# One pair of w_down's block sums made in the up projection instead of beside the last heads, in a hybrid attention and feed-forward layer on Trainium2

## The chip, the cores and the metric

The kernel runs on one core of one Trainium2 chip. The metric is the device time of one execution in microseconds (us). A core has a matrix engine (PE), a vector engine (DVE), a scalar engine (ACT), GpSimd (POOL) and SyncE (SP), which here only issues DMA transfers. Each engine works through its own list of instructions in order and waits on semaphores; a transfer that SP issues runs on 16 DMA engines that all queues share.

## The reference

One layer over 256 positions of width 2048: an RMS norm, one wide projection `w_in` (queries, keys and values for 6 forgetting heads, 6 stick-breaking heads and 4 heads over a memory, and three gates), the heads, three branch products weighted by the gates, an output product, and a gated feed-forward with a causal convolution of three taps. All in float32.

```
proj = rms_norm(x, g_mix) @ w_in
merged = g0 * (o_fox @ w_br_fox) + g1 * (o_sb @ w_br_sb) + g2 * (o_mem @ w_br_mem)
x = x + merged @ w_out
u = causal_depthwise_conv(rms_norm(x, g_ffn) @ w_up, conv_w, conv_b)
u_gate, u_val = split(u);   x = x + (silu(u_gate) * u_val) @ w_down
```

## The kernel before

**Products.** Every weight arrives as float32 in pieces of 128 x 1024 (512 KB), which SP loads into one of four `raw` buffers. ACT rounds a piece to `hi` (line 143 or 379) and DVE makes the rest, `lo = raw - hi` (line 144 or 380); there are four `hi` and four `lo` buffers. PE multiplies with `hi` and `lo` (lines 385 to 387, and 1365 and 1366 in the up stage). A `raw` buffer is free for the load of the piece four later when `lo` of its own piece is made.

**Stages**, in order of time: the memory product `kv`, the projections `mq`, `f` and `s` with the heads between them, the branch products of the first half (`b`, with the last stick-breaking heads beside them), the gates (`g`), the branch products of the second half, `w_out` (`o`), `w_up` (`u`) and `w_down` (`d`).

**Block sums.** In `w_out` and `w_down` some pairs of k-tiles ("sevens", the letter `s` in the plans) are multiplied in seven block products instead of eight. These need sums of the weight's blocks, four per pair, which do not depend on the data. A stream makes them ahead of time: it loads a pair's weights (1 MB), DVE adds them (`sums_in`, lines 254 to 256), and the sums are stored to HBM as `kept_...`, from where the `o` and `d` stages load them. The pairs stand in one list, `halves`, and generators take them from its front: `first_sums` and `pair_sums_ahead` beside the projections (15 pairs), `half_sums` (half a pair at a time, a load of two times 256 KB, three DVE operations and a store of 512 KB) beside the branch products, and `pair_sums_ahead` in the up stage (whole pairs, 18 of them).

**The up stage.** `w_up` is read in 176 steps of one piece each; eight steps fill four banks, and the order of the groups is gate columns, value columns, gate columns, and so on. After each step's matmuls `tick()` moves the background generators by one. `DU` is the number of ticks before the first pair of sums, and the tuple handed to `pair_sums_ahead` (line 1274) gives the ticks from each pair's load to the next one's. A pair's sums are written one tick after its load and its store five ticks after it. All pairs of this stage use one buffer, `ends`, so that a load waits until the store before it has landed. In the first steps ACT and DVE also end the `w_out` stage, form the transposed hidden state `hT`, and make the row scale `rbc`: DVE line 637 gives `scales`, POOL sends it to HBM and back (lines 1233 and 1234), and DVE line 1310, the first operation of each convolution after its copies, reads it.

Of the kernel before, what the change touches and what calls it, by code (L numbers as in the profile page):

```python
# [10 lines left out]
F32 = mybir.dt.float32  # L11
# [5 lines left out]
P = 128  # L17
# [19 lines left out]
BLOCKS = 14  # L37
GS = 3
PF = (6, 5)
DU = 7  # L40


@with_exitstack
def hybrid_block(
# [76 lines left out]
    def until(*names):  # L121
        while not issued.issuperset(names):
            yield
# [128 lines left out]
    def sums_in(w):  # L252
        both = w[:, 1:2].to_broadcast([P, 2, w.shape[2]])
        in_order(nc.vector.tensor_tensor(w[:, 0:2], w[:, 0:4:3], both, ALU.add))
        in_order(nc.vector.tensor_tensor(w[:, T2], w[:, T1], w[:, T2], ALU.add))
        in_order(nc.vector.tensor_tensor(w[:, T4], w[:, T2], w[:, T4], ALU.add))

    def kept_for(name, nb, pr):
        if (name, nb, pr) not in sums_of:
            at = f"kept_{name}{nb}_{pr}"  # L260
            sums_of[name, nb, pr] = dram.tile([P, 4, 512], F32, tag=at, name=at)
        return sums_of[name, nb, pr]

    def half_sums(staging, period, add, store, starts):

        for start in starts:
            yield from until(*start)
            name, wv, nb, pr, h = halves.popleft()
            kept = kept_for(name, nb, pr)
            w = staging(f"pre_{name}{nb}_{pr}_{h}").rearrange("p (i c) -> p i c", i=4)  # L270
            n0 = nb * PIECE + h * 256
            for n in range(2):
                in_order(
                    nc.sync.dma_start(
                        w.rearrange("p (k n) c -> p k n c", k=2)[:, :, n],
                        wv[:, 2 * pr : 2 * pr + 2, n0 + n * 512 : n0 + n * 512 + 256],
                    )
                )
            for _ in range(add):
                yield  # L280
            sums_in(w)
            for _ in range(store - add):
                yield
            in_order(nc.sync.dma_start(kept[:, :, h * 256 : (h + 1) * 256], w))
            for _ in range(period - store):
                yield

    def pair_sums_ahead(staging, period, add, store, most=99, delay=0):

        due = deque()  # L290
        clock = 0
        for _ in range(delay):
            yield

        def step():
            while due and due[0][0] <= clock:
                _, kept, w = due.popleft()
                in_order(nc.sync.dma_start(kept, w))

        periods = cycle(period if isinstance(period, tuple) else (period,))  # L300
        while len(halves) > 1 and halves[0][-1] == 0 and most:
            most -= 1
            name, wv, nb, pr, _ = halves.popleft()
            halves.popleft()
            kept = kept_for(name, nb, pr)
            w = staging(f"pre_{name}{nb}_{pr}")
            in_order(
                nc.sync.dma_start(
                    w.rearrange("p (k c) -> p k c", k=2), wv[:, 2 * pr : 2 * pr + 2, nb * PIECE : (nb + 1) * PIECE]
                )  # L310
            )
            w = w.rearrange("p (i c) -> p i c", i=4)
            due.append((clock + store, kept, w))
            for t in range(next(periods)):
                if t == add:
                    sums_in(w)
                step()
                clock += 1
                yield
        while due:  # L320
            step()
            clock += 1
            yield
# [342 lines left out]
    gp = mix.enter_context(tc.tile_pool(name="gp", bufs=3))  # L666
# [407 lines left out]
    def x_sums():  # L1074
# [5 lines left out]

    background.append(x_sums())
    background.append(
        half_sums(lambda name: gp.tile([P, 1024], F32, tag="pre", bufs=1, name=name), 6, 2, 4, ((), (), ("second",), ()))
    )


# [165 lines left out]
    for nb, plan in enumerate(o_plans):  # L1252
# [18 lines left out]
    ends = []  # L1271
    ends_tile = lambda name, dt: ff.tile([P, 2, PIECE], dt, tag="ends", bufs=1, name=name)
    background.append(
        pair_sums_ahead(lambda name: ends_tile(name, F32).rearrange("p i c -> p (i c)"), (15,) + (8,) * 20, 1, 5, delay=DU)
    )
    a_done = []
    background.append(last_sums(148, 12))
# [72 lines left out]
    for f0 in range(0, FT, 4):  # L1350
# [5 lines left out]
        for s in range(2):  # L1356
            ps = [bank(f"u{f0 + i}_{s}") for i in range(4)]
            c0 = s * D_FF + f0 * P
            for k in range(0, KT, 2):
                hi, lo = piece(upv[:, k : k + 2, c0 : c0 + 512], 2, 512, f"u{f0}_{s}_{k}")  # L1360
                for j in range(2):
                    first, last = k + j == 0, k + j == KT - 1
                    for i in range(4):
                        c = slice(i * P, (i + 1) * P)
# [63 lines left out]
    for nb, plan in enumerate(d_plans):  # L1428
# [5 lines left out]
        for t in range(NT):  # L1434
            for n in range(2):
                c = nb * PIECE + n * 512
                o = xres[:, t, c : c + 512]
                nc.vector.tensor_tensor(o, o, X[t][n], ALU.add)
                if (nb, t, n) == (1, 1, 1):
                    nc.scalar.dma_start(ov[:, t, c : c + 256], o[:, :256])  # L1440
                    c, o = c + 256, o[:, 256:]
# [35 lines left out]
```

## Time and profile before

| | |
|---|---|
| time, median of 3 runs | 1453.27 us (1453.22 to 1453.76) |
| profiled execution | 1453.81 us, of which the span is 1452.1 us |
| PE, DVE, ACT busy | 1447.0, 1247.5, 870.1 us |
| up stage on PE | from about 737 us on, 176 steps |
| pairs of sums in the up stage | 18 loads of 1 MB and 18 stores of 1 MB |

The span is cut into engines' busy times; a row of the timeline gives start and duration in us, engine, source line, operation, and what it writes and reads. Matmuls are pipelined: their durations overlap, so the distance from start to start tells PE's pace. SPq is the issue of a transfer, not its run.

### The profile page before, as it was taken

The page shows a single profiled execution, that of the slowest core. Times are in us where ns is not written, and L with a number is a line of the kernel's source. Part 1 is how long each engine was busy: PE and PEld are TensorE (multiplying, and loading weights), DVE is VectorE, ACT ScalarE, POOL GpSimd, SP SyncE. Part 2 cuts the span into 40 slices and gives each one's busy share as a digit, 9 for nine tenths or more (in the row PEclk, how much of TensorE's full clock was granted, in tenths as well). Part 3 has the DMA queues.
Part 4 walks back from the last instruction along what each step waited for, and adds up shares of the span by engine and source line. Part 5 has one row for each costly group of instructions (what it writes and reads, how often), then busy time and mean ns, then how long its engine had stood idle before and what let it go on. Part 6 is the DMA issues. An engine that isn't in the chain of part 4 may idle for free.

```text
span 1452.1 us, 20709 instructions
## 1 busy us (share of the span) xinstructions
PE 1447.0 (100%) x7298; PEld 1225.8 (84%) x7298; DVE 1247.5 (86%) x1851; ACT 870.1 (60%) x1248; POOL 32.3 (2%) x70
## 2 busy tenths in 40 slices
PE   9999999999999999999999999999999999999998
PEld 7888888888888888888888888888888888888887
DVE  5888778777999999998897888888888877999988
ACT  6755445465555555546676656556556556676775
POOL 0000011010000000000000000000000011000000
PEclk9999999999999999999999999999999999999999
DMA  8797899775677676788877888888888899789996
GB/s 296 228 350 269 309 336 321 266 250 182 214 219 230 202 219 207 265 267 278 289 231 264 302 273 292 284 267 303 288 275 298 274 252 262 251 286 345 317 341 236
DMA packets 165783, 393.41 MB, mean 271 GB/s; under 512 B 12859, under 2 KB 28111, under 8 KB 161327
## 3 DMA queue, kind: packets, MB, share of 16 engines
q1 hardware_dynamic: 162190, 384.86, 79.3%
q0 software_dynamic: 2160, 5.12, 1.8%
q10 hardware_dynamic: 1328, 2.11, 0.4%
q8 instruction: 57, 0.93, 0.2%
q14 instruction: 48, 0.39, 0.1%
HBM read 353.24 MB, written 43.00 MB: 273 GB/s over the span
## 4 chain that ended last, share of the span: by engine, by line
PE 98%; DMA 1%; ACT 0%; DVE 0%; issue 0%; DVEq 0%; ACTq 0%
PE u L1365 22%; PE u L1366 11%; PE xg L387 5%; PE xg L386 5%; PE xg L385 5%; PE xd L387 3%; PE xd L386 3%; PE xd L385 3%; PE s L385 2%; PE s L387 2%; PE f L385 2%; PE f L386 2%; PE f L387 2%; PE s L386 2%; PE b L387 2%; PE b L386 2%
## 5 line engine op out<-in xcount | busy, mean ns | idle before, releaser
L1365 PE MATMUL u<-hT,hi_u 128*128 128x512 f32 x1232 | 428.4, 394 | 0.0
L1366 PE MATMUL u<-hT,lo_u 128*128 128x256 f32 x1232 | 341.3, 277 | 0.0
L1365 PEld LDWEIGHTS u<-hT,hi_u 128*128 128x128 f32 x1232 | 231.0, 188 | 53.6
L144 DVE TENSOR_TENSOR lo_u<-raw_u,hi_u 128x1024 fp32r<-128x1024 f32 x176 | 215.1, 1222 | 69.4 <-ACT hi_u L143 69.3
L143 ACT CAST hi_u<-raw_u 128x1024 fp32r<-128x1024 f32 x176 | 184.6, 1050 | 131.5 <-PE u L1365 105.1
L1366 PEld LDWEIGHTS u<-hT,lo_u 128*128 128x128 f32 x1232 | 231.3, 188 | 0.0
L379 ACT CAST hi_g<-raw_g 128x1024 fp32r<-128x1024 f32 (+1 forms) x96 | 92.5, 973 | 54.0 <-PE xg L386 23.7
L380 DVE TENSOR_TENSOR lo_d<-raw_d,hi_d 128x1024 fp32r<-128x1024 f32 x88 | 106.8, 1222 | 12.3 <-ACT hi_d L379 6.9
L379 ACT CAST hi_d<-raw_d 128x1024 fp32r<-128x1024 f32 x88 | 91.7, 1054 | 35.8 <-PE xd L386 12.2
L380 DVE TENSOR_TENSOR lo_g<-raw_g,hi_g 128x1024 fp32r<-128x1024 f32 (+1 forms) x96 | 106.4, 1119 | 4.1 <-ACT hi_g L379 3.6
L385 PE MATMUL xg<-hi_g,xT 128*128 128x512 f32 x210 | 82.0, 390 | 0.0
L387 PE MATMUL xg<-lo_g,xT 128*128 128x512 f32 x210 | 81.8, 389 | 0.0
L386 PE MATMUL xg<-hi_g,xT 128*128 128x512 f32 x210 | 81.7, 389 | 0.0
L379 ACT CAST hi_t_g<-t_g 128x1024 fp32r<-128x1024 f32 x36 | 37.9, 1053 | 48.7 <-PE xg L386 41.4
L143 ACT CAST hi_f<-raw_f 128x1024 fp32r<-128x1024 f32 (+1 forms) x40 | 38.6, 968 | 39.9 <-PE f L386 23.7
L1365 PE MATMUL u<-hT_rest,hi_u 128*128 128x512 f32 x176 | 62.0, 394 | 0.0
L144 DVE TENSOR_TENSOR lo_s<-raw_s,hi_s 128x1024 fp32r<-128x1024 f32 (+1 forms) x40 | 44.6, 1123 | 18.5 <-ACT hi_s L143 18.5
L1315 ACT ACTIVATE y<-u,taps 128x256 f32<-128x256 f32 x88 | 49.6, 596 | 17.5 <-DVE u L1310 17.4
L143 ACT CAST hi_s<-raw_s 128x1024 fp32r<-128x1024 f32 (+1 forms) x40 | 38.3, 960 | 32.5 <-PE s L386 19.5
L380 DVE TENSOR_TENSOR lo_t_g<-t_g,hi_t_g 128x1024 fp32r<-128x1024 f32 x36 | 43.6, 1221 | 14.7 <-ACT hi_t_g L379 14.6
L144 DVE TENSOR_TENSOR lo_f<-raw_f,hi_f 128x1024 fp32r<-128x1024 f32 (+1 forms) x40 | 44.4, 1117 | 13.8 <-ACT hi_f L143 13.6
L379 ACT CAST hi_t_d<-raw_t_d 128x1024 fp32r<-128x1024 f32 (+1 forms) x54 | 43.5, 835 | 19.1 <-PE xd L386 11.7
(556 smaller groups left out, 3496.3 us busy)
## 6 DMA issues: line engine op xcount, KB each, us to landing
raw_u<-in_w_up_dram SPq DMA_DIRECT2D x176, 512.0 KB, 5.0
raw_g<-in_w_in_dram SPq DMA_DIRECT2D x96, 512.0 KB, 4.4
raw_d<-in_w_down_dram SPq DMA_DIRECT2D x61, 512.0 KB, 5.6
pre_d<-in_w_down_dram SPq DMA_DIRECT2D x18, 1024.0 KB, 7.4
kept_d<-pre_d SPq DMA_DIRECT2D x18, 1024.0 KB, 6.1
raw_f<-in_w_in_dram SPq DMA_DIRECT2D x32, 512.0 KB, 5.8
raw_s<-in_w_in_dram SPq DMA_DIRECT2D x32, 512.0 KB, 6.1
raw_t_d<-kept_d SPq DMA_DIRECT2D x27, 512.0 KB, 6.7
```

Source lines behind the costliest of these rows:

```text
L143: pin(nc.scalar.copy(hi[:, :m], raw[:, :m]))
L144: pin(nc.vector.tensor_tensor(lo[:, :m], raw[:, :m], hi[:, :m].bitcast(F32), ALU.subtract))
L379: nc.scalar.copy(hi[:, :n], src)
L380: nc.vector.tensor_tensor(lo[:, :n], src, hi[:, :n].bitcast(F32), ALU.subtract)
L385: fix(nc.tensor.matmul(o, lhsT=ah, rhs=w[0], start=first, stop=False))
L386: fix(nc.tensor.matmul(o, lhsT=al, rhs=w[0], start=False, stop=False))
L387: fix(nc.tensor.matmul(o, lhsT=ah, rhs=w[1], start=False, stop=last))
L1315: nc.scalar.activation(y, u[:, 2:], AF.Identity, scale=tap(2), bias=tap(3))
L1365: nc.tensor.matmul(ps[i], lhsT=hi[:, j, c], rhs=hT(k + j), start=first, stop=False)
L1366: nc.tensor.matmul(ps[i][:, :S], lhsT=lo[:, j, c], rhs=hT(k + j)[:, :S], start=False, stop=last)
```

## The change

Two tables of numbers change. `half_sums` now makes two half pairs, both after the gates of the second half ("second"), and not four, so the pair that it made beside the last heads and the first half's branch products is left for the next generator. In the up stage the first load comes after 6 ticks and not 7, the second 7 ticks later, and the third 9 ticks after that, at tick 22 as before; from there on the ticks of the loads are the same. The stage makes 19 pairs. Since pairs are taken from the front of a list, the pair called d0_5 is now made where d0_6 was, and d0_6 is the new first pair of the up stage.

```diff
-DU = 7
+DU = 6
...
-        half_sums(lambda name: gp.tile([P, 1024], F32, tag="pre", bufs=1, name=name), 6, 2, 4, ((), (), ("second",), ()))
+        half_sums(lambda name: gp.tile([P, 1024], F32, tag="pre", bufs=1, name=name), 6, 2, 4, (("second",), ()))
...
-        pair_sums_ahead(lambda name: ends_tile(name, F32).rearrange("p i c -> p (i c)"), (15,) + (8,) * 20, 1, 5, delay=DU)
+        pair_sums_ahead(lambda name: ends_tile(name, F32).rearrange("p i c -> p (i c)"), (7, 9) + (8,) * 20, 1, 5, delay=DU)
```

PE's and POOL's lists are the same before and after. SP's list in the up stage moves as follows. `raw_u_0_14` is step 7 (gate columns, k-tiles 14 and 15), `raw_u_1_0` is step 8 (value columns), and the `raw_u_0_0` after it step 16; `pre_d` is a pair's load and `kept_d` its store. In brackets stands what the issue waits for; DMAHW is the landing of an earlier transfer. Before, steps 7 to 13 with the only pair of the first sixteen steps:

```order
L142 DMA raw_u_0_14_7076<-in_w_up_dram 128x2x512 [waits DMAHW4_49,DVE_49]
L308 DMA pre_d_7_7099<-in_w_down_dram 128x2x1024 [waits PE_49]
L142 DMA raw_u_1_0_7105<-in_w_up_dram 128x2x512 [waits DMAHW5_49,DVE_49]
L142 DMA raw_u_1_2_7140<-in_w_up_dram 128x2x512 [waits DMAHW6_49,DVE_49,Activation_49]
L142 DMA raw_u_1_4_7168<-in_w_up_dram 128x2x512 [waits DMAHW7_49,DVE_49]
L142 DMA raw_u_1_6_7190<-in_w_up_dram 128x2x512 [waits DMAHW0_49,DVE_49]
L478 DMA raw_t_d_0_12107<-kept_d_0_2285 128x512
L478 DMA raw_t_d_1_12198<-kept_d_1_2443 128x512
L142 DMA raw_u_1_8_7212<-in_w_up_dram 128x2x512 [waits DMAHW2_49,DVE_49]
L142 DMA raw_u_1_10_7235<-in_w_up_dram 128x2x512 [waits DMAHW3_49,DMAHW1_49,DVE_49]
L298 DMA kept_d_7_7098<-pre_d_7_7099 128x2048 [waits DVE_49]
```

Now, from the first pair's store on:

```order
L298 DMA kept_d_6_7061<-pre_d_6_7062 128x2048 [waits DVE_49]
L142 DMA raw_u_1_10_7220<-in_w_up_dram 128x2x512 [waits DMAHW5_49,DVE_49]
L142 DMA raw_u_1_12_7245<-in_w_up_dram 128x2x512 [waits DMAHW6_49,DVE_49]
L308 DMA pre_d_7_7243<-in_w_down_dram 128x2x1024 [waits DMAHW3_49]
L142 DMA raw_u_1_14_7275<-in_w_up_dram 128x2x512 [waits DMAHW7_49,DMAHW1_49,DVE_49]
L142 DMA raw_u_0_0_7306<-in_w_up_dram 128x2x512 [waits DMAHW2_49,DMAHW0_49,DVE_49]
L142 DMA raw_u_0_2_7333<-in_w_up_dram 128x2x512 [waits DMAHW4_49,DVE_49]
L142 DMA raw_u_0_4_7371<-in_w_up_dram 128x2x512 [waits DMAHW5_49,DVE_49]
L142 DMA raw_u_0_6_7394<-in_w_up_dram 128x2x512 [waits DMAHW7_49,DVE_49]
L298 DMA kept_d_7_7242<-pre_d_7_7243 128x2048 [waits DMAHW6_49,DVE_49]
```

The first store now stands ahead of step 13's load and not behind it, and the second pair's load stands ahead of step 15's, waiting for the landing (DMAHW3) of that store. The first pair's load stands one row earlier than before, between steps 6 and 7.

DVE's list at the row scale (lines 635 to 637) and the first pair's sums (254 to 256), before:

```order
L144 TENSOR_TENSOR lo_u_0_14_7078<-raw_u_0_14_7076,hi_u_0_14_7077 128x1024
L635 TENSOR_TENSOR nwt_f<-nwy_f 128x2
L636 SCALAR_TENSOR_TENSOR nwt_f<-nwt_f,nwa_f 128x2
L637 SCALAR_TENSOR_TENSOR scales<-nwt_f,nwy_f 128x2
L144 TENSOR_TENSOR lo_u_1_0_7107<-raw_u_1_0_7105,hi_u_1_0_7106 128x1024
L254 TENSOR_TENSOR pre_d_7_7099<-pre_d_7_7099 128x1024
L255 TENSOR_TENSOR pre_d_7_7099<-pre_d_7_7099 128x512
L144 TENSOR_TENSOR lo_u_1_2_7142<-raw_u_1_2_7140,hi_u_1_2_7141 128x1024
L256 TENSOR_TENSOR pre_d_7_7099<-pre_d_7_7099 128x512
```

and now:

```order
L144 TENSOR_TENSOR lo_u_0_14_7066<-raw_u_0_14_7064,hi_u_0_14_7065 128x1024
L254 TENSOR_TENSOR pre_d_6_7062<-pre_d_6_7062 128x1024
L635 TENSOR_TENSOR nwt_f<-nwy_f 128x2
L255 TENSOR_TENSOR pre_d_6_7062<-pre_d_6_7062 128x512
L636 SCALAR_TENSOR_TENSOR nwt_f<-nwt_f,nwa_f 128x2
L144 TENSOR_TENSOR lo_u_1_0_7095<-raw_u_1_0_7093,hi_u_1_0_7094 128x1024
L637 SCALAR_TENSOR_TENSOR scales<-nwt_f,nwy_f 128x2
L256 TENSOR_TENSOR pre_d_6_7062<-pre_d_6_7062 128x512
L144 TENSOR_TENSOR lo_u_1_2_7127<-raw_u_1_2_7125,hi_u_1_2_7126 128x1024
```

The sums now stand between the operations of the row scale, whose last one (637) comes behind step 8's `lo`. The second pair's sums are new in DVE's list, behind step 14's `lo` and ahead of the first convolution's line 1310:

```order
L144 TENSOR_TENSOR lo_u_1_12_7247<-raw_u_1_12_7245,hi_u_1_12_7246 128x1024
L254 TENSOR_TENSOR pre_d_7_7243<-pre_d_7_7243 128x1024
L255 TENSOR_TENSOR pre_d_7_7243<-pre_d_7_7243 128x512
L144 TENSOR_TENSOR lo_u_1_14_7277<-raw_u_1_14_7275,hi_u_1_14_7276 128x1024
L256 TENSOR_TENSOR pre_d_7_7243<-pre_d_7_7243 128x512
L1310 TENSOR_TENSOR u_7115<-y_0_7119,rbc 128x256
```

Before, line 1310 followed step 14's `lo` directly, and step 15's `lo` came after three operations of the first convolution.

## The prediction

> **What bounds the kernel now.** I read the page first: the span, the engines' shares and the chain that ended last.
>
> ```profile
> span 1452.1 us, 20709 instructions
> PE 1447.0 (100%) x7298; PEld 1225.8 (84%) x7298; DVE 1247.5 (86%) x1851; ACT 870.1 (60%) x1248; POOL 32.3 (2%) x70
> PE 98%; DMA 1%; ACT 0%; DVE 0%; issue 0%; DVEq 0%; ACTq 0%
> ```
>
> PE is idle for 1452.1 - 1447.0 = 5.1 us in all, and the chain is PE for 98%. But durations of pipelined matmuls overlap, so a busy PE may still wait. Hence the second view, the timeline of PE: steps 16 and 24 of the up stage, each with its first `hi` and its first `lo` matmul.
>
> ```profile
> 783.33 0.39 PE L1365 MATMUL u<-hT,hi_u 128*128 128x512 f32 x1
> 783.56 0.27 PE L1366 MATMUL u<-hT,lo_u 128*128 128x256 f32 x1
> 805.51 0.39 PE L1365 MATMUL u<-hT,hi_u 128*128 128x512 f32 x1
> 805.75 0.27 PE L1366 MATMUL u<-hT,lo_u 128*128 128x256 f32 x1
> ```
>
> Eight steps take 805.51 - 783.33 = 22.18 us for 128 matmuls, or 2.77 us a step. Third, the busy time by stretch (columns: length, then busy us and count of PE, PEld, DVE, ACT, POOL; clock, DMA share, GB/s): heads with the first branch products, the end of `w_out`, and `w_down`.
>
> ```profile
> 300.00:331.00 31.00, 31.00 (x175) 27.33 (x174) 26.66 (x42) 21.76 (x36) 1.91 (x7) 1.00 0.90 307
> 700.00:737.00 37.00, 36.89 (x171) 30.46 (x170) 31.98 (x39) 27.79 (x41) 0.00 (x0) 1.00 0.80 263
> 1200.00:1452.00 252.00, 248.38 (x1139) 206.92 (x1137) 226.29 (x324) 164.60 (x220) 3.54 (x5) 1.00 0.87 291
> ```
>
> Of the 5.1 us, 3.6 lie in the last stretch, 0.1 at the end of `w_out`, and none beside the heads. So the sum is simple: PE's list is unchanged, and the time changes only by PE waits that go or come.
>
> **What is removed.** One pair in two halves, with DVE operations like these of the second half:
>
> ```profile
> 327.39 0.69 DVE L254 TENSOR_TENSOR pre_d<-pre_d 128x512 f32<-128x512 f32 x1
> 328.12 0.42 DVE L255 TENSOR_TENSOR pre_d<-pre_d 128x256 f32<-128x256 f32 x1
> 328.57 0.43 DVE L256 TENSOR_TENSOR pre_d<-pre_d 128x256 f32<-128x256 f32 x1
> L385 PE MATMUL b<-hi_b,oT 128*128 128x512 f32 x128 | 50.3, 393 | 0.0
> L387 PE MATMUL b<-lo_b,oT 128*128 128x512 f32 x128 | 49.9, 390 | 0.0
> L386 PE MATMUL b<-hi_b,oT 128*128 128x512 f32 x128 | 49.8, 389 | 0.0
> ```
>
> Per half 0.69 + 0.42 + 0.43 = 1.54 us, so 3.1 us of DVE, 1 MB of loads and 1 MB of stores leave this place. What can PE get back? A wait for a piece would stretch its first matmul, line 385. It takes 393 ns against 389 to 390 for the other two: at most 4 ns x 128 = 0.5 us over both halves' branch products, other causes included. Bounds 0 to -0.5 us; I take 0, because PE is busy for 31.00 of 31 us there.
>
> PEld is busy for 27.33 of those 31 us. The Trainium skill (Perfetto Trace Analysis, Identifying the Most-Contended Engine) says that matmul busy time tells little and that weight-load busy time is the measure of headroom; by it this place would have 3.7 us to give, and the sum here could be up to -3.1 us, all of DVE's work. The 4 ns above do not bear that out.
>
> **The first pair of the up stage, one step earlier.** Its load waits for the last reader of a buffer in the memory that it takes over, and stands ahead of step 7's load:
>
> ```profile
> 741.33 0.68 DVE L422 TENSOR_TENSOR xres_again<-xres_again,e 128x512 f32<-128x512 f32 x1
> 743.60 0.81 SPq L308 DMA_DIRECT2D pre_d<-in_w_down_dram  x1
> 756.46 3.38 SPq L142 DMA_DIRECT2D raw_u<-in_w_up_dram  x2
> 760.06 0.34 SPq L298 DMA_DIRECT2D kept_d<-pre_d  x1
> pre_d<-in_w_down_dram SPq DMA_DIRECT2D x18, 1024.0 KB, 7.4
> kept_d<-pre_d SPq DMA_DIRECT2D x18, 1024.0 KB, 6.1
> ```
>
> It can go at 741.33 + 0.68 = 742.0 and not at 743.60, and lands 7.4 us later, at 749.4, before DVE comes to it. Cost 0. The sums:
>
> ```profile
> 754.27 0.16 DVE L635 TENSOR_TENSOR nwt_f<-nwy_f 128x2 f32<-128x2 f32 x1 [1.81 <-ACT nwy_f L634]
> 756.35 1.22 DVE L254 TENSOR_TENSOR pre_d<-pre_d 128x1024 f32<-128x1024 f32 x1
> 757.60 0.69 DVE L255 TENSOR_TENSOR pre_d<-pre_d 128x512 f32<-128x512 f32 x1
> 759.34 0.69 DVE L256 TENSOR_TENSOR pre_d<-pre_d 128x512 f32<-128x512 f32 x1
> 755.11 0.74 POOL L1233 DMA_DIRECT2D rstd_row<-scales  x1 [418.96 <-DVE scales L637]
> 763.94 0.56 POOL L1234 DMA_DIRECT2D rbc<-rstd_row  x1 [8.09 <-DMA rstd_row<-scales]
> 775.02 0.42 DVE L1310 TENSOR_TENSOR u<-y,rbc 128x256 f32<-128x256 f32 x1
> ```
>
> A pair costs DVE 1.22 + 0.69 + 0.69 = 2.6 us. Line 254 now fills the 1.81 us in which DVE waited for ACT; the other two delay `scales`, so the row goes out some 2 us later, near 757, and is back by 2 us later too. Its first reader, line 1310 at 775.02, now stands behind the new sums anyway. Cost 0, while `rbc` lands before about 776. The store can go at about 757.4 (step 12's load, 756.46, then the end of line 256), 2.7 us sooner than 760.06.
>
> **The second pair: its load.** It waits for that store's landing, and behind it on SP stand the loads of steps 15 and later. What lies there now is a slump of the DMA engines:
>
> ```profile
> 760.00:764.00 4.00, 4.00 (x25) 3.52 (x24) 3.71 (x7) 2.29 (x5) 0.06 (x1) 1.00 0.50 38
> 768.00:772.00 4.00, 4.00 (x25) 3.52 (x24) 2.17 (x2) 1.05 (x1) 0.00 (x0) 1.00 1.00 401
> 766.64 1.05 ACT L143 CAST hi_u<-raw_u 128x1024 fp32r<-128x1024 f32 x1 [4.05 <-DMA raw_u<-in_w_up_dram]
> 768.76 1.05 ACT L143 CAST hi_u<-raw_u 128x1024 fp32r<-128x1024 f32 x1 [1.08 <-DMA raw_u<-in_w_up_dram]
> 772.80 1.05 ACT L143 CAST hi_u<-raw_u 128x1024 fp32r<-128x1024 f32 x1 [2.98 <-DMA raw_u<-in_w_up_dram]
> ```
>
> They move 38 GB/s in 760 to 764, while the scale's row is under way (POOL waits 8.09 us for it), and 401 GB/s in 768 to 772. Step 12's piece, issued at 756.46, is there at 766.6 only. At 401 GB/s a 1 MB transfer takes 2.6 us of the queue and a piece 1.3; steps 13 and 14 start 4.04 us apart on ACT, with the store between them: 2.6 + 1.3 = 3.9 agrees.
>
> Now the store lies behind step 12's piece. If the slump stays where it is, it lands at 766.6 + 2.6 = 769.2; if it moves with the scale's row, step 12 is early and the store lands 2.6 us after a slump that ends near 767, at 769.6. I take 769.5. SP issues the new load then (0.81), step 15 at 770.3 and step 16 at 770.7. The queue: steps 13 and 14 by 772.2, the 1 MB load by 774.8, step 15 by 776.1, step 16 by 777.4. Step 15's `hi` is made by 776.1 + 1.05 = 777.2; PE begins the step at 783.33 - 2.77 = 780.56, so 3.4 us are spare. Cost 0, with a wait on SP of about 9 us that the `raw` buffers cover.
>
> **The second pair: its sums.** They are new between steps 14 and 16 of DVE's list. Step 16's and step 24's `lo` now, and DVE around them:
>
> ```profile
> 776.00:780.00 4.00, 4.00 (x25) 3.52 (x24) 3.14 (x6) 3.97 (x6) 0.00 (x0) 1.00 0.54 148
> 780.00:784.00 4.00, 4.00 (x25) 3.48 (x24) 4.00 (x8) 3.10 (x5) 0.00 (x0) 1.00 0.59 200
> 780.22 1.23 DVE L144 TENSOR_TENSOR lo_u<-raw_u,hi_u 128x1024 fp32r<-128x1024 f32 x1
> 802.12 1.22 DVE L144 TENSOR_TENSOR lo_u<-raw_u,hi_u 128x1024 fp32r<-128x1024 f32 x1
> ```
>
> PE reads step 16's `lo` at 783.56, 2.11 us after it is made (780.22 + 1.23); step 24's at 805.75, 2.41 us after 803.34. In the new order: lines 254 and 255 after the landing, 774.8 + 1.9 = 776.7; step 15's `lo` at 777.2 to 778.4, needed at 780.8; then 256 and two of line 1310 until about 779.9, and step 16's `lo` until 781.1, needed at 783.56: 2.5 us spare. But the four convolutions have been pushed behind it, and from 780 on DVE has no idle time. The new work is 2.6 us; idle time of 4 - 3.14 = 0.86 us before 780 takes some. So step 24 comes between 2.6 - 0.86 = 1.7 and 2.6 us later, and against 2.41 us that is 0.7 us spare to 0.2 us of stall. Where a reordered operation waits for ACT as well, I allow half the new work again, 1.3 us: bounds 0 and 1.5 us, and I take 0.3, near the rows of DVE alone. Behind step 20 DVE's list is as before; what PE loses up to there it does not get back.
>
> **Sum.** 0 + 0 + 0 + 0.3 us on the profiled execution's 1453.81 us. That lies 0.54 us over the median of the runs, 1453.27, against which I state it: 1453.27 + 0.3 = 1453.6 us; with the bounds -0.5 and +1.5, 1452.8 to 1454.8.
>
> **Rivals.** (1) *SP is held too long*: slower. If the store lands x us after 769.5, all behind it moves by x. The least spare is step 15's `lo`, 780.8 - 778.4 = 2.4 us, so it decides from a landing at 771.9 on, one for one. A slump of 14.4 us where about 8 were waited now (POOL's 8.09) gives x = 6.4, a loss of 4.0 us: 1457.3. For it: pieces took 10 us there, and the store writes in the slump. Against: at the median landing of 6.1 us, 757.4 + 6.1 = 763.5, SP hardly waits, and PE never ran dry in the slump so far. (2) *The branch products gain what DVE is spared*: 1453.27 - 3.1 = 1450.2. For it: DVE is busy for 26.66 of 31 us there, and PE takes its `lo` pieces. Against: 31.00 of 31 us and the bound of 0.5 us. The measure of headroom on the page Perfetto Trace Analysis of the Trainium skill would allow it. (3) *DVE's backlog costs more than the bound*, because the third pair's sums meet it before step 24: the whole 2.6 us beyond the spare, 2.6 us, 1455.9, still within what can be told apart.
>
> **How the numbers follow.** About 0.2% (2.9 us) is what a measurement can tell from no change here. Chances: the forecast 0.82, rival 1 0.10, rival 2 0.03, rival 3 0.05. Faster 0.03; the same 0.82 + 0.05 = 0.87; slower 0.10. The range takes in the bounds and rival 3 and leaves out rivals 1 and 2, 0.13 together: 1452.7 to 1455.9.
>
> **What would show it.** In the profile after: PE 31 of 31 us beside the heads as before; the new load issued near 769 to 770 and a gap in SP's issues before it; step 15's and 16's `lo` made 2 us or more before their matmuls; step 24's nearly late. I am wrong if line 1365 or 1366 stands idle for over 1.5 us between steps 12 and 30, or if PE before 700 us ends earlier by more than 0.5 us.

## The result, and the profile after

| | before | after |
|---|---|---|
| time, median of 9 runs each | 1453.35 us (1452.82 to 1454.04) | 1464.53 us (1457.69 to 1468.14) |
| profiled execution | 1453.81 us, span 1452.1 us | 1458.11 us, span 1456.4 us |

The ratio of all executions is 1.0061 with a 95% interval of 1.0042 to 1.008 (the medians alone give 1.0077): the changed kernel is slower. The prediction said 1453.6 us and no change. The nine times after lie in two groups, four at 1457.69 to 1458.11 us and five at 1464.53 to 1468.14 us; the profiled execution belongs to the first. So there are two things to explain: 4.3 us in the profile, and some 6 to 10 us more in the second group.

The head of the page after:

```profile
span 1456.4 us, 20700 instructions
PE 1448.8 (99%) x7298; PEld 1229.4 (84%) x7298; DVE 1247.9 (86%) x1848; ACT 870.0 (60%) x1248; POOL 32.5 (2%) x70
```

PE's busy time grew by only 1448.8 - 1447.0 = 1.8 us, so 4.3 - 1.8 = 2.5 us of the difference are idle time. Now the place that the pair left: two stretches of the busy times after, heads with the first branch products and the end of `w_out` (columns as in the prediction):

```profile
300.00:331.00 31.00, 31.00 (x175) 27.33 (x175) 24.17 (x35) 22.41 (x38) 2.39 (x8) 1.00 0.81 272
700.00:737.00 37.00, 37.00 (x173) 30.88 (x172) 33.68 (x41) 28.21 (x42) 0.00 (x0) 1.00 0.82 277
```

DVE is busy for 24.17 us and not 26.66 beside the heads, and PE for 31.00 of 31 us as before: nothing to win. The 0.1 us of idle time at the end of `w_out` is gone.

The loss lies in the up stage. These rows of PE's timeline are the first matmuls of steps 12 and 30, before:

```profile
772.24 0.39 PE L1365 MATMUL u<-hT,hi_u 128*128 128x512 f32 x1
822.15 0.39 PE L1365 MATMUL u<-hT,hi_u 128*128 128x512 f32 x1
```

and after, with the waits between them:

```profile
772.00 0.39 PE L1365 MATMUL u<-hT,hi_u 128*128 128x512 f32 x1
774.77 0.39 PE L1365 MATMUL u<-hT,hi_u 128*128 128x512 f32 x1
775.48 0.39 PE L1366 MATMUL u<-hT,lo_u 128*128 128x256 f32 x1 [0.32 <-DVE lo_u L144]
780.89 0.28 PE L1366 MATMUL u<-hT,lo_u 128*128 128x256 f32 x1
781.70 0.49 PE L1365 MATMUL u<-hT_rest,hi_u 128*128 128x512 f32 x1 [0.53 <-ACT hi_u L143]
782.96 0.39 PE L1366 MATMUL u<-hT_rest,lo_u 128*128 128x256 f32 x1 [0.77 <-DVE lo_u L144]
808.54 0.40 PE L1365 MATMUL u<-hT,hi_u 128*128 128x512 f32 x1
809.66 0.39 PE L1366 MATMUL u<-hT,lo_u 128*128 128x256 f32 x1 [0.72 <-DVE lo_u L144]
826.19 0.39 PE L1365 MATMUL u<-hT,hi_u 128*128 128x512 f32 x1
```

Eighteen steps took 822.15 - 772.24 = 49.91 us and take 826.19 - 772.00 = 54.19 us: 4.3 us, which is the whole difference of the two profiled executions. PE waits at step 13 (774.77), twice at step 15 (780.89 and 781.70), a little at step 18, and at step 24 (808.54). From start to start these five gaps are 3.3 us longer than the usual distances; the other 1.0 us is a slower pace between them, to which the last experiments come back. The idle time in brackets adds up to 2.3 us in these steps; over 1.5 us between steps 12 and 30 was the prediction's sign of being wrong.

Why the pieces are late is seen in the timeline of POOL, SP, ACT and DVE after:

```profile
756.56 0.74 POOL L1233 DMA_DIRECT2D rstd_row<-scales  x1 [421.70 <-DVE scales L637]
772.12 0.56 POOL L1234 DMA_DIRECT2D rbc<-rstd_row  x1 [14.82 <-DMA rstd_row<-scales]
756.90 0.34 SPq L298 DMA_DIRECT2D kept_d<-pre_d  x1
758.03 2.89 SPq L142 DMA_DIRECT2D raw_u<-in_w_up_dram  x2
772.06 0.37 SPq L308 DMA_DIRECT2D pre_d<-in_w_down_dram  x1
773.12 1.05 ACT L143 CAST hi_u<-raw_u 128x1024 fp32r<-128x1024 f32 x1 [8.31 <-DMA raw_u<-in_w_up_dram]
780.60 1.05 ACT L143 CAST hi_u<-raw_u 128x1024 fp32r<-128x1024 f32 x1 [5.16 <-DMA raw_u<-in_w_up_dram]
779.26 1.23 DVE L254 TENSOR_TENSOR pre_d<-pre_d 128x1024 f32<-128x1024 f32 x1 [2.56 <-DMA pre_d<-in_w_down_dram]
780.52 0.69 DVE L255 TENSOR_TENSOR pre_d<-pre_d 128x512 f32<-128x512 f32 x1
781.68 1.23 DVE L144 TENSOR_TENSOR lo_u<-raw_u,hi_u 128x1024 fp32r<-128x1024 f32 x1 [0.46 <-ACT hi_u L143]
```

The scale's row goes out at 756.56 and the store 0.34 us behind it, at 756.90. POOL then waits 14.82 us for the row (8.09 before), and SP 11 us for the store, until 772.06. The DMA view of 750 to 785 us shows what the queues did meanwhile; its line of GB/s has 40 slices of 0.875 us. Before:

```profile
GB/s 356 379 391 91 131 346 396 315 54 61 33 101 28 35 47 14 56 262 309 318 452 407 393 386 405 407 405 410 300 115 161 363 59 56 236 307 0 94 353 208
```

After:

```profile
GB/s 262 262 332 309 297 377 131 2 84 119 353 464 385 197 129 47 30 44 96 47 35 49 30 138 215 344 255 276 426 328 138 136 321 403 410 410 407 346 129 105
```

Before, nine slices from the ninth on (14 to 61 GB/s, one at 101) are slow: 757.0 to 764.9 us; this is the slump of the prediction. After, 353 to 464 GB/s move first, and the slow slices are the sixteenth to the twenty-third (30 to 49, one at 96): 763.1 to 770.1 us. The records of single packets say what moved first: the store's 8 KB packets. Before, they ran behind the slump, from 766 to 771 us; after, they started at 759.5 us, 104 of the 128 ended ahead of it, and the rest inside it, the last at 770.6 us. The row's own first packets ran 1.6 us behind its issue before, and 3.9 us behind it after, 0.9 us behind the store's first. All 16 packets of the row (64 bytes each) start by 757.2 us before and by 761.8 us after, so the records do not say what fills the slump. **The slump is no longer than before; it begins 6 us later, behind the store.** Step 13's piece, issued at 758.03, is caught in it and is there at 773.12; PE is at step 13 at 774.77 and finds its `lo` unmade.

### The profile page after: what moved, and what is told of

The parts are those of the page before. It is cut to its first block, busy times and chain, and to the rows that moved or that the text cites. A ratio compares the mean times of both kernels' runs of the same rounds, so it can differ in the third digit from the quotient of the medians.

```text
span 1456.4 us, 20700 instructions
## 1 busy us (share of the span) xinstructions
PE 1448.8 (99%) x7298; PEld 1229.4 (84%) x7298; DVE 1247.9 (86%) x1848; ACT 870.0 (60%) x1248; POOL 32.5 (2%) x70
## 4 chain that ended last, share of the span: by engine, by line
PE 96%; DMA 2%; DVE 1%; ACT 1%; issue 0%; SPq 0%; ACTq 0%; DVEq 0%
PE u L1365 20%; PE u L1366 10%; PE xg L385 5%; PE xg L386 5%; PE xg L387 5%; PE xd L385 3%; PE xd L387 3%; PE xd L386 3%; PE s L387 2%; PE s L385 2%; PE f L385 2%; PE f L387 2%; PE f L386 2%; PE s L386 2%; PE b L385 2%; PE b L387 2%
## 5 line engine op out<-in xcount | busy, mean ns | idle before, releaser
L1366 PE MATMUL u<-hT,lo_u 128*128 128x256 f32 x1232 | 345.1, 280 | 1.1 <-DVE lo_u L144 1.0
L380 DVE TENSOR_TENSOR lo_t_g<-t_g,hi_t_g 128x1024 fp32r<-128x1024 f32 x36 | 43.6, 1220 | 14.4 <-ACT hi_t_g L379 14.3
```

Source lines behind the costliest of these rows:

```text
L380: nc.vector.tensor_tensor(lo[:, :n], src, hi[:, :n].bitcast(F32), ALU.subtract)
L1366: nc.tensor.matmul(ps[i][:, :S], lhsT=lo[:, j, c], rhs=hT(k + j)[:, :S], start=False, stop=last)
```

## The experiments

### What makes the slump, and what the store has to do with it

*No row.* The changed kernel without the write of the scale's row; `rbc` is loaded from `g_mix` instead, so its values are not the layer's, and everything else is in its place.

```diff
-            row = dram.tile([NT, P], F32, tag="rstd_row", name="rstd_row")
-            nc.gpsimd.dma_start(row.rearrange("t p -> p t"), rstd_f)
-            nc.gpsimd.dma_start(rbc, row.rearrange("t p -> (t p)").partition_broadcast(P))
+            nc.gpsimd.dma_start(rbc, g_mix[0][:S].partition_broadcast(P))
```

> The changed kernel, but the scale's row is not written to HBM: rbc is loaded at the start from 256 values of g_mix, so the output is not the reference's. All other lists of instructions are as in the changed kernel. Theory 1 (the row's 4-byte writes and the pair's store, which now stands ahead of them, make a long slump of the DMA engines, and pieces and store land late): no slump, kept_d_6 lands about 6 us after its issue, 1453.0 to 1454.0 us. Theory 2 (SP held by the second pair's load until the store lands, in whatever slump): also back to 1453 to 1454, since the hold ends early. Theory 3 (2.6 us more of DVE between steps 14 and 24): the stall at step 24 stays, 1454 to 1456. If the slump has nothing to do with the row's writes, 1458 to 1468 as in the changed kernel.

Measured: 1455.43 us (1454.54 to 1457.48, 10 runs) where the kernel before took 1453.98 us, ratio 1.0009 [1.0, 1.0017]. PE does not wait in the up stage, and the DMA view of the same 35 us has no slump:

```profile
GB/s 403 346 372 318 265 281 351 314 260 115 47 84 272 487 421 412 363 368 372 382 417 407 391 405 393 283 367 140 77 309 213 35 63 255 480 403 421 375 391 300
```

(Its three slices of 115, 47 and 84 lie ahead of the store's first packet, as 131, 2, 84 and 119 do in the profile after.) Steps 12 to 30 take 49.92 us. So without the row all of the change's loss in the up stage is gone, although store, load and sums stand where the change put them. The time alone would also fit theory 3, 1454 to 1456 us; that there is no wait at step 24 decides against it. The profiled execution, at 1455.86 us, lost its 2 us ahead of the first branch product, which starts at 309.34 us and not at 307.10; in all the profiles this start varies from 306.85 to 310.65 us, in a part that the change leaves as it is. The row is two values on each of 128 partitions, written as 4-byte elements to HBM. The Trainium skill (DMA: Bandwidth & Descriptors, Specifications) says that a transfer below 512 bytes is done by reading, modifying and writing; that would fit a slump of everything beside such a row, but no run here shows that it is the cause.

*First pair early.* The kernel before, with the first pair of the up stage one tick earlier and nothing else: the pair beside the heads stays, and there is no second pair in the first sixteen steps.

```diff
-DU = 7
+DU = 6
...
-(15,) + (8,) * 20
+(16,) + (8,) * 20
```

> The kernel before with one part of the change alone: the first pair of the up stage one tick earlier (6 and not 7), the second at tick 22 as before, so no second pair in the first sixteen steps and nothing on SP waits for the first store there. Theory 1: the store stands ahead of the row's writes, POOL waits over 12 us for the row and not 8, pieces of steps 13 to 16 land late: 1454 to 1460 us. Theories 2 and 3: 1453.3 us, within 0.5.

Measured: 1455.33 us (1454.26 to 1465.39, 12 runs), ratio 1.0024 [1.0008, 1.0041]. Its SP and POOL rows:

```profile
759.29 0.34 SPq L298 DMA_DIRECT2D kept_d<-pre_d  x1
758.96 0.74 POOL L1233 DMA_DIRECT2D rstd_row<-scales  x1 [421.62 <-DVE scales L637]
774.39 0.55 POOL L1234 DMA_DIRECT2D rbc<-rstd_row  x1 [14.70 <-DMA rstd_row<-scales]
```

Again the store stands 0.33 us behind the row, and POOL waits 14.70 us. So the earlier store alone delays the slump. But PE lost only some 0.8 us in waits here: what comes on top in the changed kernel needs the second pair.

*Two ticks later.* The changed kernel with both pairs moved by two ticks, so that the first store stands clear behind the row.

```diff
-DU = 6
+DU = 8
...
-(7, 9) + (8,) * 20
+(7, 7) + (8,) * 20
```

> The changed kernel with its pairs of the first sixteen steps at ticks 8 and 15 and not 6 and 13 (third at 22 as before): the first store, at tick 13, now comes behind the writes of the scale's row, the rest of the change stays. Slump theory (store ahead of the row's 4-byte writes makes the slump long): POOL waits about 8 us for the row and not 15, no wait at steps 13 and 15, at most 0.9 us at step 24: 1453.5 to 1456, unless the pace turns slow. If it is the second pair as such that costs, 1458 to 1468 as in the changed kernel.

Measured: 1455.33 us (1453.53 to 1464.09, 11 runs; before: 1453.74 us), ratio 1.0018 [1.0004, 1.0033]. Store and row are 7 us apart:

```profile
754.59 0.74 POOL L1233 DMA_DIRECT2D rstd_row<-scales  x1 [420.01 <-DVE scales L637]
763.99 0.56 POOL L1234 DMA_DIRECT2D rbc<-rstd_row  x1 [8.66 <-DMA rstd_row<-scales]
761.75 0.34 SPq L298 DMA_DIRECT2D kept_d<-pre_d  x1
773.42 0.37 SPq L308 DMA_DIRECT2D pre_d<-in_w_down_dram  x1
```

POOL waits 8.66 us, and steps 12 to 30 take 49.92 us with no wait of PE in this execution (at 1453.53 us), though this kernel too has two pairs in its first sixteen steps, the second one's load even later than in the changed kernel. So the second pair costs nothing where it stands there, two steps later.

*No pair near.* The kernel before with its first pair 7 ticks later (`DU = 14`, `(8,) + (8,) * 20`): no pair's store until 782.20 us. (Its load is issued at 761.95 us, while POOL waits for the row.)

> The kernel before with the up stage's first pair loaded at tick 14 and not 7 (second at 22 as before), so that no load or store of a pair is under way when the scale's row is written. Slump theory: POOL's wait for the row falls from 8.09 us to 3 to 6 us, or stays near 8 if the 4-byte writes alone make it; time 1453.3 to 1454.5 either way. If the slump has nothing to do with the pair's transfers in either kernel, the wait stays within 7.5 to 8.5 us.

Measured: 1454.7 us (1453.37 to 1462.53, 10 runs), ratio 1.0017 [1.0002, 1.0032]; POOL waits 8.54 us, PE does not wait. All kernels together, by the distance from the row's issue to the store's:

| kernel | row out, us | store out, us | POOL waits for the row, us |
|---|---|---|---|
| no pair near | 755.85 | 782.20 | 8.54 |
| two ticks later | 754.59 | 761.75 | 8.66 |
| before | 755.11 | 760.06 | 8.09 |
| spread (below) | 758.25 | 763.19 | 7.72 |
| after | 756.56 | 756.90 | 14.82 |
| load on POOL (below) | 757.12 | 757.46 | 15.11 |
| first pair early | 758.96 | 759.29 | 14.70 |

In further executions of the kernels "no pair near" and "after" (below) the wait is 9.38 us and 13.41 to 14.07 us. So a store of 1 MB issued a third of a microsecond behind the row adds 4 to 7 us to the wait; a store 5 us behind it adds nothing. No distance in between was tried.

### Is it the hold on SP?

*Load on POOL.* The changed kernel with the second pair's load issued by POOL, so that SP holds no step's load behind it.

```diff
-                nc.sync.dma_start(
+                (nc.gpsimd if (name, nb, pr) == ("d", 0, 7) else nc.sync).dma_start(
```

> The changed kernel with the second pair's load issued by POOL and not by SP: it still waits for the first store's landing, but the loads of steps 15 and later do not stand behind it. Theory 1 (long slump, pieces of steps 13 and 14 land late whatever SP does): a stall at step 13 stays, 1454.5 us and more, up to 1465. Theory 2 (SP held): steps 15 and 16 are issued near 763 to 766, no stall over 0.5 us, 1453.3 to 1454.0. Theory 3 (DVE): 1454 to 1456 with the stall at step 24 alone.

Measured: 1463.01 us (1459.1 to 1469.19, 6 runs), ratio 1.0062 [1.0038, 1.0086]: as slow as the changed kernel. Its ACT and DVE rows at step 15:

```profile
776.69 1.05 ACT L143 CAST hi_u<-raw_u 128x1024 fp32r<-128x1024 f32 x1 [0.21 <-DMA raw_u<-in_w_up_dram]
780.85 1.23 DVE L254 TENSOR_TENSOR pre_d<-pre_d 128x1024 f32<-128x1024 f32 x1 [3.12 <-DMA pre_d<-in_w_down_dram]
782.11 0.69 DVE L255 TENSOR_TENSOR pre_d<-pre_d 128x512 f32<-128x512 f32 x1
782.72 1.22 DVE L144 TENSOR_TENSOR lo_u<-raw_u,hi_u 128x1024 fp32r<-128x1024 f32 x1
```

With SP free, step 15's piece is there by 776.69, 4 us sooner than in the changed kernel, and it helps nothing: its `lo` stands in DVE's list behind the pair's sums, which wait for the pair's load until 780.85. So it is not SP's hold alone; the same late load also blocks DVE's list. PE waits here 1.72 us at step 15, 0.97 us at step 13 and 0.89 us at step 24.

The edit does more than free SP, though. In POOL's list the load stands behind that of `rbc`, which waits for the row: it was issued at 773.91 us and not at 772.06, and landed 1.6 us later than in the changed kernel. What SP's hold is worth is better read in the changed kernel itself: there DVE was through with line 255 at 781.2 us and stood idle for 0.46 us, until `hi` of the piece that SP had issued at 772.53 was made. Without the hold, by these rows, step 15's `lo` could have begun those 0.46 us sooner; the rest of the 1.7 us that PE loses at step 15 there is the late load's, by way of DVE's list.

### The removal alone

*Spread.* The changed kernel's `half_sums` (no pair beside the heads) with the first store as before; the missing pair is made up by closer periods later in the stage.

```diff
-DU = 6
+DU = 7
...
-(7, 9) + (8,) * 20
+(15,) + (8, 8, 8, 7) * 5
```

> The changed kernel's other part alone: no pair beside the last heads, and the up stage's 19 pairs spread over the whole stage (first at tick 7, second at 22, then every 8, 8, 8 and 7 ticks), so the first sixteen steps are as before. All theories: no stall, 1453.3 us within 0.5; below 1452.5 only if the pair beside the last heads had cost PE something.

Measured: 1458.82 us (1457.47 to 1460.21, 7 runs), ratio 1.0028 [1.0017, 1.0038]. The first branch product to the first matmul of `w_up` takes 429.59 us, as in the changed kernel (429.60) and in the kernel with the first pair early, which still has the pair beside the heads (429.61). So the removal is worth nothing. (The kernel before needs 430.01 in its profile, with a short wait at the end of `w_out`, and the kernel with no pair near 429.89; a second execution of the latter, with the pair beside the heads like both, needs 429.59, so this wait does not belong to the pair.)

The time missed what was expected of it by 5 us. PE's first sixteen steps have no wait, but the up stage takes 3.0 us more: waits of 0.2, 1.2 and 0.3 us near 1112, 1154 and 1177 us, where the later pairs now stand closer, and a slower pace from 1066.6 us to the first of them. So a 19th pair is not free there either. Another 3.5 us of the profiled execution lie ahead of the first branch product, in a part that the change leaves as it is.

### Where the rest of the median comes from

*Added work on DVE.* The kernel before, with five added DVE operations (each takes the maximum of `xres` with itself, 128 x 1024, 1.22 us) in DVE's list at steps 40 and 41 (shown), or at steps 152 and 153, to make PE wait once at a place far from the slump. PE's list is as before but for a few matmuls of the two steps behind, whose `hi` products now stand ahead of their `lo` products.

```diff
+                for _ in range(5 if (f0, s, k) == (8, 0, 4) else 0):
+                    in_order(nc.vector.tensor_tensor(xres[:, 0, :1024], xres[:, 0, :1024], xres[:, 0, :1024], ALU.max))
```

> The kernel before with five operations more on DVE (a maximum of a residual tile with itself, 128 x 1024, which changes no value, 1.13 us from start to start) in step 40 and 41 of the up stage, and nothing else: they make `lo` late by up to 5.7 us against about 4 us spare, so PE waits 0.5 to 2 us once. Pace theory (after a wait PE goes on in the up stage at one of two paces, 2.773 or 2.827 us a step, and keeps it to the end of the stage): some executions at 1454 to 1456.5, others later by 135 steps x 0.053 = 7.2 us, 1461 to 1464. Rival (a wait costs its own length only): all executions at 1454 to 1456.5.

> The same five operations at steps 152 and 153. Pace theory: 24 steps are left, so the slow pace adds 1.3 us at most: all executions between 1454 and 1458. Rival (a wait costs its own length only): the same times as with the wait at step 40.

Measured: at step 40 1462.68 us (1456.06 to 1464.68, 6 runs), ratio 1.0051 [1.0033, 1.0069]; at step 152 1463.64 us (1462.58 to 1464.56, 4 runs), ratio 1.0066 [1.0053, 1.0079]. The second missed what was expected of it: there PE waited 5.8 us at once, at 1167.85 us, because ACT in turn waited 4.10 us for a piece of `w_up`, so the wait itself is most of the 9 us. Behind it PE goes on at 2.773 us a step, and behind a wait of 0.2 us at 1202.8 us at 2.827: a longer wait is not what leaves the slower pace. The kernel with the wait at step 40 ran once more:

> The kernel before with five added DVE operations at steps 40 and 41 once more; its first profile, at 1464.68 us, had waits of some 4.6 us at 852 to 862 us and 2.827 us a step behind them. Theory of two paces: an execution near 1456 to 1458 us has the same waits and 2.773 us a step behind them, so that pace and waits are two things; at 1462 to 1465 us it shows 2.827 again. Rival (the pace is nothing but the waits' own size): the pace behind the waits is the same at either time, and the waits differ by 6 us and more.

This execution took 1463.99 us. It has one wait in the stage, and these are its PE rows at the wait and at the first matmuls of steps 60 and 100 (line 1367 is line 1365 of the kernel before):

```profile
859.31 0.39 PE L1368 MATMUL u<-hT,lo_u 128*128 128x256 f32 x1 [1.97 <-DVE lo_u L144]
909.36 0.40 PE L1367 MATMUL u<-hT,hi_u 128*128 128x512 f32 x1
1022.42 0.40 PE L1367 MATMUL u<-hT,hi_u 128*128 128x512 f32 x1
```

The same two steps in the profile after:

```profile
909.39 0.39 PE L1365 MATMUL u<-hT,hi_u 128*128 128x512 f32 x1
1020.32 0.39 PE L1365 MATMUL u<-hT,hi_u 128*128 128x512 f32 x1
```

Forty steps take 113.06 us here, 2.827 us a step, and 110.93 us there, 2.773 us a step, with no wait in either and a granted clock of 1.00 in both. Ahead of its wait this same execution goes at 2.773 us a step too: steps 12 to 30 take 49.92 us. One wait of 2.1 us has cost 9.1 us by step 170: 2.1 at its place and 7.0 in 128 steps at the slower pace. The execution of the kernel with the first pair early that was profiled, at 1465.39 us, shows the same: 2.827 us a step from 786.5 us to the end of the stage, 8.5 us in all. An execution of the kernel with the added work at 1456 to 1458 us, which would go on at 2.773 us a step by this theory, was not profiled.

*The changed kernel again.* Five more executions of it, unchanged, and one more of the kernel with no pair near, each with its trace.

> The changed kernel once more, unchanged, for the trace of an execution other than the one at 1458.11 us. Theory (PE has two paces in the up stage, 2.773 and 2.827 us a step, and some executions fall into the second one after a wait and stay there): steps 12 to 30 take 54 us as before; if the time is 1458 us, steps 30 to 170 take 388.3 us; if it is 1465 to 1468 us, they take about 395.8 us, spread evenly, with no single wait over 1 us. Rival (the longer executions have a second row of waits on pieces of w_up, or a longer slump): steps 30 to 170 stay at 388.3 us outside a few waits of 1 us and more, or steps 12 to 30 take over 60 us.

> The same kernel and the same alternatives as the look before it: 388.3 us for steps 30 to 170 at a time near 1458 us, about 395.8 us spread evenly at 1465 to 1468 us.

> The changed kernel unchanged, for the trace of an execution at 1464 us or more. Theory of two paces: there steps 30 to 170 of the up stage take about 395.8 us (2.827 us a step, evenly), and steps 12 to 30 still 53 to 55 us. Rival (more waits): steps 30 to 170 take 388.3 us but for single waits of 1 us and more, or steps 12 to 30 take over 60 us. An execution near 1458 us says nothing more than the looks before it.

> As the look before it: at 1464 us or more, steps 30 to 170 at about 395.8 us evenly by the theory of two paces, waits of 1 us and more by the rival.

> As the two looks before it: at 1464 us or more, steps 30 to 170 at about 395.8 us evenly by the theory of two paces, single waits of 1 us and more by the rival.

> The kernel before with its first pair taken out of the reach of the slump (load 761.95 us, store 782.2 us) once more: three of its ten executions took 1461.3 to 1462.5 us, and the one profiled, at 1454.55 us, had no wait of PE in the up stage. Theory of the two paces: at 1461 to 1463 us steps 30 to 170 take 394 to 396 us evenly; near 1454 us they take 388.3 us. Rival: a wait of several us at one place.

Measured: 1459.11, 1457.57, 1456.77, 1457.6 and 1456.86 us, all by the first group, and 1453.8 us, where PE did not wait in the up stage. In the five, steps 12 to 30 take 54.55, 52.87, 52.94, 53.40 and 52.97 us, and steps 30 to 170 388.27 us each, as before. POOL waits 13.41 to 14.07 us. So the first part, 3.0 to 4.6 us of waits and of a slower pace between them, is there in each of the six profiles of the changed kernel; of its second group no trace exists. In the execution at 1459.11 us the clock granted to PE was half for 3.4 us from 783.65 us on, behind the waits at steps 14 and 15. Half of that, 1.7 us, is about what its steps 12 to 30 take more than those of the others (1.2 to 1.7 us). The clock does not tell the two groups apart: over the whole execution it is 0.999 in the first, and 0.999 or 1.0 in four of the five of the second, 0.997 at 1468.14 us. The kernel with the load on POOL has two such groups too, three executions at 1459.10 to 1459.19 us and three at 1466.83 to 1469.19 us.

What the profiles do show is where the pace changes. In the profile after, PE's stretch between two of the waits, from the matmul at 791.72 us to the one at 808.54 us, as a row of the busy times (length, busy us and count of PE; clock, DMA share, GB/s):

```profile
791.72:808.54 16.82, 16.82 (x95) 1.00 0.77 252
```

These are 95 matmuls in 16.82 us, 177 ns each or 2.83 us a step; behind the next wait, at 809.66, it is 173.3 ns each, 2.773 us a step, to the end. In one of the five further executions PE goes at 2.83 us a step there too, in the other four at 2.773. The wait near 809 us found PE at one pace or the other and left it at 2.773 us a step in all six. Were it left at 2.827, the 152 steps from there on would take 152 x 0.054 = 8.2 us more: 1458.1 + 8.2 = 1466.3 us, the middle of the second group. That the five executions at 1464.53 us and above are these is the likeliest reading, but it is not shown.

A change of pace does not even need a wait that the profile shows. These are rows of the spread kernel: the first matmul of step 107, the `lo` of step 117 on DVE, the first two matmuls of step 117, and the first of step 132.

```profile
1038.83 0.39 PE L1365 MATMUL u<-hT,hi_u 128*128 128x512 f32 x1
1065.34 1.23 DVE L144 TENSOR_TENSOR lo_u<-raw_u,hi_u 128x1024 fp32r<-128x1024 f32 x1
1066.57 0.40 PE L1365 MATMUL u<-hT,hi_u 128*128 128x512 f32 x1
1066.80 0.28 PE L1366 MATMUL u<-hT,lo_u 128*128 128x256 f32 x1
1108.97 0.40 PE L1365 MATMUL u<-hT,hi_u 128*128 128x512 f32 x1
```

Ten steps up to step 117 take 27.74 us, 2.774 each, and fifteen from there on 42.40 us, 2.827 each. At the turn no wait stands, only a `lo` made at 1066.57 us, 0.23 us before its matmul. In all 17 profiles of this stage, from step 8 on, every change of pace stands at a step with a wait or with a `lo` that was made within 0.3 us of its matmul; the 3 to 7 us at half the granted clock, behind long waits in three of them, are left out of this.

## Why the prediction was wrong

**What held.** The removal gains nothing: the forecast was 0 (bounds 0 to -0.5 us), and 429.60 us against 429.61 with the pair in place says 0. The measure of headroom of the Trainium skill (Perfetto Trace Analysis, Identifying the Most-Contended Engine), by which up to 3.1 us could have come, was no sign of what this removal gives: PEld is busy for 27.33 us of 31 both with and without the pair, and PE gets nothing back. The sums of the first pair went as worked out, and so did the row (756.56 us, forecast near 757) and the store (756.90, forecast 757.4).

**The step that failed** is the one on the second pair's load: "If the slump stays where it is, it lands at 766.6 + 2.6 = 769.2; if it moves with the scale's row, step 12 is early and the store lands 2.6 us after a slump that ends near 767, at 769.6", and before it, of the row, "is back by 2 us later too". Both cases let the slump come first, soon after the row's issue, and the store behind it. In fact the store, issued 0.34 us behind the row, ran ahead for the most part, and the slump came behind it, 6 us later than before. From there every number of that part is late:

| | forecast, us | measured, us |
|---|---|---|
| scale's row back | near 766 | 772.1 |
| second pair's load issued | 769.5 | 772.06 |
| steps 13 and 14 landed | by 772.2 | 773.1 and 774.4 |
| second pair landed | 774.8 | 779.26 |
| step 15's `lo` begins | 777.2 | 781.68 |

The load took 779.26 - 772.06 = 7.2 us from its issue where I allowed 774.8 - 769.5 = 5.3 us: the slices from 771.9 to 778.9 us (344 to 321) are 278 GB/s on the mean and not 401. Step 15's `lo` was to have 2.4 us to spare and begins 4.5 us later than forecast. Where the sum had 0.3 us for the whole change, the profile lost 4.3. The rows that were there did not exclude it: they showed the slump only with the store 4.95 us behind the row, and I moved the store to the row without a bound for how the two go together.

**Rival 1** came nearest. It gave a slump of 14.4 us and 1457.3 us; POOL's wait is 14.82 us and the profile 1458.11 us. But that its loss of 4.0 us lies so near the 4.3 us of the profile is luck. By its own formula a store landed at 772.06 costs 772.06 - 771.9 = 0.2 us, the hold on SP is worth at most 0.46 us at step 15, and with SP free the loss stays. What costs is the later slump itself (step 13) and DVE's list standing behind the late load (step 15).

**The second pair's sums**, the only term that was not zero, were sized at 0.3 us at step 24. PE's gap there is 0.9 us too long, with DVE's backlog as the releaser, inside the bounds of 0 to 1.5.

**The chances.** The forecast and all three rivals supposed that PE's pace is one number. The second group, which decides the median, comes from nothing in the sum: I priced a wait at its own length, and in this stage a wait of 2 us has been seen to cost 9.

Still open: why the store goes ahead of the row when it follows this closely; what fills the slump; which wait leaves PE at which pace; and why two of eleven executions with the pairs two ticks later and three of ten with no pair near took 1461.3 us and more, when no wait was seen in their profiles. There the least time between a `lo` and its matmul, from step 8 on, is 1.1 and 1.2 us, against 2.1 us in the kernel before, so they are nearer to a change of pace; none of the longer executions was profiled, so this is not shown. None of 60 executions of the kernel before went above 1457 us. No version tried beats the kernel before.

## What to carry to other kernels

A dip in what the DMA engines move belongs to the transfer that makes it, not to a time: before moving another transfer next to that one, ask what order the two will take, and give the dip's new place a price as well as its length. Where operations of two streams stand in one engine's list, the late load of one holds the other back even if the queue that issues the loads is free. And a chain that is all matmul can have more than one pace: look at the distance of matmuls behind the last wait, not only at the waits, and at how late each operand is made.

## What was not expected of the hardware

- A 1 KB row written as 4-byte elements goes with 7 to 10 us in which all queues together move 0 to 105 GB/s (slices of 0.875 us); without the row they move 272 to 487 GB/s from the store's first packets on.
- A 1 MB store issued 0.33 to 0.34 us behind that row lengthens the wait for the row from 7.7 to 9.4 us to 13.4 to 15.1 us; one issued 5 or 7 us behind it does not.
- PE runs the same list of matmuls at 2.773 or at 2.827 us a step, at a granted clock of 1.00, and changes between them only at a wait or where a `lo` is made within 0.3 us of its matmul.
